# An encoder trunk on one core: the first two chunks of the input projection run side by side, and x, weights and the residual share one queue

## The chip, the core and the metric

The kernel runs on one core of a Trainium2 chip. A core has engines that each work through their own instructions in order: TensorE (PE: matmuls, with PEld its weight loads), VectorE (DVE), ScalarE (ACT), GpSimd (POOL) and SyncE (SP). SP, ACT and POOL also issue transfers (DMA) between the chip's memory and the core's own memory; a transfer that has to wait for something holds up whatever stands behind it on the engine that issues it. Matmul results collect in eight banks (PSUM). The metric is the device time of one execution in microseconds; the number given is the median of several runs.

## The reference

Two encoder layers on 256 tokens of width 2048, in float32. Each layer has an attention part and an MLP part, each ahead of a norm over the width. Layer 0 uses differential attention (12 heads, two softmaxes subtracted), layer 1 windowed attention with a sink; in both, four more heads attend to 256 memory tokens. A relative-position bias table is shared. Cut to what matters here:

```
h = rms_norm(x, norm_attn[i])
proj = h @ w_in_a[j]                              # 2048 x 5120 in layer 0
q, k, v, q_m = split(proj, [1536, 3072, 4608])
q = rms_norm(q per head half, a_q_norm[j]);  k = rms_norm(k per head half, a_k_norm[j])
o = diff_attention(q, k, v, positions, rel_bias, lam, 64 ** -0.5)
...
x = x + heads @ w_out[i]
h = rms_norm(x, norm_mlp[i])
x = x + square(relu(h @ w_up[i])) @ w_down[i]
```

## The kernel before

**Precision.** Every float32 factor is split into a rounded part `hi` and a rest `lo`, and a product is made of three matmuls: x_hi w_hi, x_hi w_lo, x_lo w_hi. For weights, ScalarE makes `hi` (L184) and VectorE `lo` (L185); for x, ScalarE multiplies by the norm's gain and rounds (L200) and VectorE makes the rest (L201). The norm's factor per token is not needed for that; it is applied to the results, from statistics over the tokens (`row_stats`, into `st0`).

**Weights.** Every weight matrix is cut into chunks of 512 columns, and each chunk into eight pieces of 512 KB: 128 partitions x 1024 floats, which are two k tiles (128 rows of the contraction each) of 512 columns. `plan` lists all pieces in the order of use; `fetch` takes the next one, issues its transfer on SP's queue (L183) and its two conversions; `piece` keeps up to three pieces fetched (AHEAD = 2). The raw piece, `hi` and `lo` have four buffers each.

**A chunk of a projection** (`chunk_tok`) takes two banks, one for each 128 tokens, and for each piece runs 2 k tiles x 2 token tiles x 3 matmuls = 12 matmuls (L276 to L278). Eight pieces make 96 matmuls.

**The first chunk** (chunk 6 of layer 0, values of the first four heads) is special: `lead=first` makes each piece come in two halves of 256 KB, and before each half prepares one k tile of x: `load_x` issues the transfers of x on ScalarE's queue (L724; block 0 in two parts of 128 KB, the others, two k tiles each, 256 KB), and `make_x2` converts. So during the first chunk all of x and the chunk's weights have to arrive. The second chunk (chunk 0, queries) needs only weights.

**The residual.** `xt`, x by tokens, is loaded in four parts of 512 KB on SP's queue (L730, task `loads`), each placed behind the last weight transfer (`issue_after(behind[0])`). From it come the statistics: `chunk_sq` (L234) four times, then `start_stats`, which also copies the value chunk out of its banks.

**Side work.** A list of `Task`s holds everything that isn't a chunk: `tick` counts one and runs the first task step that is due and whose predecessors are done; `tick(2)` runs two. Each piece ends with a tick. Tasks of the start: the scalars (L589 to L602), the preparation of the position bias (`prep`: seven steps, among them position transfers L511 and L513, arithmetic on VectorE from L518, and the table written to memory at L535), eight pairs `bias_hot` (four spread loads on GpSimd's queue, L560, and a comparison, L562) and `bias_rows` (48 small matmuls, L571, into two "aux" banks, copied out by VectorE and ScalarE, L572), then the norms and transposes of q and k (`norm_T`) and the attention heads. PSUM has four banks with the tag "mm" and four with "aux".

A scheduler of the framework places the instructions of each engine, mostly in program order; it can place one that it holds to be ready ahead of one that still waits. Ahead of everything 16 warm-up products run on TensorE (L99; 32 matmul records).

Of the kernel before, what the change touches and what calls it, by code (L numbers as in the profile page):

```python
# [14 lines left out]
F32 = mybir.dt.float32  # L15
# [4 lines left out]
ALU = mybir.AluOpType  # L20
AX = mybir.AxisListType

P = 128
S = 256
D = 2048
KT = D // P
# [7 lines left out]
AHEAD = 2  # L34
# [3 lines left out]
G_ATTN, G_MEM, G_MLP = 0, 2 * KT, 4 * KT  # L38
# [8 lines left out]
def trunk(ctx: ExitStack, tc: tile.TileContext, xin, xtok, memin, pos, rel, gcol, rows,  # L47
          w_a, w_b, w_mem, w_out, w_up, w_down, out):
    nc = tc.nc
# [3 lines left out]
    xp = ctx.enter_context(tc.tile_pool(name="xp", bufs=1))  # L53
# [16 lines left out]
    def blk(shape, dt):  # L70
        return xp.tile(shape, dt, tag="blk", name=nm("blk"), bufs=10)
# [96 lines left out]
    ready = deque()  # L168
    behind = [None]

    def fetch(parts=1, lead=None):

        name, c, j = plan.popleft()
        src = weights[name][c, j]
# [3 lines left out]
        n = 1024 // parts  # L178
        for i in range(parts):
            s = slice(i * n, (i + 1) * n)  # L180
            if lead is not None:
                lead(i)
            behind[0] = nc.sync.dma_start(raw[:, s], src[:, s])  # L183
            nc.scalar.copy(hi[:, s], raw[:, s])  # L184
            nc.vector.tensor_tensor(lo[:, s], raw[:, s], as32(hi)[:, s], op=ALU.subtract)  # L185
        ready.append(((name, c, j), hi, lo))

    def piece(name, c, j, lead=None):

        if lead is not None:  # L190
            fetch(2, lead)
        else:
            while plan and len(ready) <= AHEAD:
                fetch()
        key, hi, lo = ready.popleft()
        assert key == (name, c, j), (key, name, c, j)
        return hi, lo
# [44 lines left out]
    def row_stats(st):  # L242
        e1 = mean_sq()
        nc.vector.tensor_scalar_mul(st[:, 0:2], e1, EPS)
        inv_sqrt(st[:, 2:4], e1, 2)
# [15 lines left out]

        return Task([lambda: two(0), lambda: two(1)], wait=1, gap=1)

    def chunk_tok(w, c, X2, before=None, lead=None, steps=1):
        ps = [bank("mm") for _ in range(2)]
        for j in range(8):
            if before is not None:
                before(j)
            hi, lo = piece(w, c, j, lead and (lambda i: lead(2 * j + i)))
            for kk in range(2):  # L270
                for t in range(2):
                    k = 2 * j + kk
                    ws = slice(kk * 512, kk * 512 + 512)
                    xh = X2[k][:, 0, t * P:(t + 1) * P]
                    xl = X2[k][:, 1, t * P:(t + 1) * P]
                    nc.tensor.matmul(ps[t], lhsT=xh, rhs=hi[:, ws], start=(k == 0), stop=False)  # L276
                    nc.tensor.matmul(ps[t], lhsT=xh, rhs=lo[:, ws], start=False, stop=False)  # L277
                    nc.tensor.matmul(ps[t], lhsT=xl, rhs=hi[:, ws], start=False, stop=(k == KT - 1))  # L278
            tick(steps)
        return ps  # L280

    def chunk_out(w, c, nj, x2_of, tag, steps=1):
        ps = [bank(tag) for _ in range(4)]
# [28 lines left out]
    def norm_T(ps, st, nseg, g, before=None):  # L312

        dim = 512 // nseg
        qn = []
        hi = blk([P, 4, S], F32R)
        lo = blk([P, 4, S], F32R)

        def rows():
            ms = small(2 * nseg)  # L320
            rs = small(2 * nseg)
            for t in range(2):
                sq = t2k([P, 512])
# [395 lines left out]
    def load_x(j):  # L719
        if j < 8:  # L720
            xs[j] = xp.tile([P, 2, S], F32, tag="h2", name=nm("xs"), bufs=12)
            for k in range(2 * j, 2 * j + 2) if j == 0 else (2 * j,):
                n = 1 if j == 0 else 2
                nc.scalar.dma_start(xs[j][:, k - 2 * j:k - 2 * j + n, :],  # L724
                                    xin[:, S * k:S * (k + n)].rearrange("p (k s) -> p k s", s=S))

    def load_residual(c):
        cs = slice(c * 512, (c + 1) * 512)
        with tc.issue_after(behind[0].ins):
            nc.sync.dma_start(xt[:, :, cs], xtok.rearrange("p (t d) -> p t d", t=2)[:, :, cs])  # L730

    def first(k):
        if k == 0:
            load_x(0)
        elif k == 1:
            load_x(1)
            load_x(2)
        elif k % 2 == 0:
            load_x(k // 2 + 2)
        X2[k] = make_x2(xs[k // 2][:, k % 2, :], gc[:, G_ATTN + k:G_ATTN + k + 1])  # L740

    bias = big([P, 12, 2, S])
    Task([scalars], wait=4)
# [2 lines left out]
    rows_done = [Task([lambda i=i: bias_hot(i), lambda i=i: bias_rows(i, bias)], [prep], wait=BW) for i in range(8)]  # L746
    Task([lambda: bias_save(bias)], rows_done)
    H2 = [None] * KT
    loads = Task([lambda c=c: load_residual(c) for c in range(4)], wait=5, gap=2, front=True)
    for g in range(3):  # L750
        ps = chunk_tok("a", 6 + g, X2, lead=first if g == 0 else None)
        steps = 2 if g == 0 else 1
        v = blk([P, 2, 512], F32)
        if g == 0:
            def start_stats(v=v, ps=ps):
                row_stats(st0)
                val_f32(v, ps, st0)

            Task([lambda c=c: chunk_sq(c) for c in range(4)] + [start_stats], (loads,), gap=1, front=True)
        else:  # L760
            val_f32(v, ps, st0)
        ps = chunk_tok("a", g, X2, steps=steps)
        qT, qd = norm_T(ps, st0, 8, gs[:, 0:1])
        ps = chunk_tok("a", 3 + g, X2)
        kT, kd = norm_T(ps, st0, 8, gc[:, G_AK:G_AK + 1])
        for h in range(4):
            Task(diff_head(h, qT, kT, v, bias, H2, 4 * g + h), [qd, kd] + rows_done)
    ps = chunk_tok("a", 9, X2)
    qm, qd = norm_T(ps, st0, 4, gs[:, 2:3])
    mem_part(0, qm, qd, H2)  # L770
# [79 lines left out]
```

## Time and profile before

| | us |
|---|---|
| median of 3 runs (lowest to highest) | 2149.51 (2148.49 to 2150.24) |
| profiled execution | 2150.42 |
| its span | 2148.6 |
| TensorE busy in the span | 2137.6 |
| VectorE, ScalarE, GpSimd busy | 1315.6, 1083.6, 35.7 |
| granted TensorE clock | 1.0 |
| moved by transfers | 409.24 MB, mean 190 GB/s |

The span runs from the first to the last instruction of the profiled execution; the execution's own time lies a little over it. Lines of the profile name the source line (L277), the engine, the operation, the output and the inputs by their names in the kernel (`mm<-lo,x`: a matmul into a bank tagged "mm" from `lo` and x), the shapes, the count, and where given the idle time of the engine just before, with what ended it. "raw" is a weight piece as it arrives, "xs" a block of x, "xt" the residual, "rw" the scalars' rows.

### The profile page before, as it was taken

Reading aid. Unit: us, or ns where it says so; the run is one execution under the profiler, and the core shown is the slowest. Engines: PE = TensorE matmul, PEld = TensorE weight load, DVE = VectorE, ACT = ScalarE, POOL = GpSimd, SP = SyncE. Lnnn points to the kernel's source line nnn. Section 1 sums busy time; section 2 is a strip of 40 time slices with the busy share of each in tenths; the row PEclk is TensorE's granted clock in tenths of the full one; section 3 lists DMA queues with packets and bytes.
Section 4 is the critical chain, followed back from the end, with each engine's and each line's share of the span. In section 5 each row is a group of like instructions: output and inputs, shape, how many; then the busy total and the mean of one; then the engine's idle time right before and its main releaser. Section 6 shows DMA issues by size and latency. Waiting matters only on the chain.

```text
span 2148.6 us, 29416 instructions
## 1 busy us (share of the span) xinstructions
PE 2137.6 (99%) x11116; PEld 1806.4 (84%) x11116; DVE 1315.6 (61%) x2067; ACT 1083.6 (50%) x1740; POOL 35.7 (2%) x61
## 2 busy tenths in 40 slices
PE   9999999999999999999999999999999999999999
PEld 7877878888888888888888888888888888888887
DVE  7667786565555555566556677655555556556554
ACT  6456675454444445555545566554444444544443
POOL 1200020000000000000000000000000000000000
PEclk9999999999999999999999999999999999999999
DMA  8865565666666666666656656566666666666654
GB/s 292 237 209 154 157 195 153 187 183 189 185 194 188 191 186 193 193 195 235 198 194 192 181 167 178 155 183 183 185 195 188 192 189 185 196 196 212 192 193 148
DMA packets 114959, 409.24 MB, mean 190 GB/s; under 512 B 13568, under 2 KB 14336, under 8 KB 114560
## 3 DMA queue, kind: packets, MB, share of 16 engines
q1 hardware_dynamic: 111840, 401.01, 60.9%
q0 software_dynamic: 1536, 4.20, 0.8%
q10 hardware_dynamic: 1440, 2.15, 0.3%
q8 instruction: 87, 1.43, 0.3%
q14 instruction: 56, 0.46, 0.1%
HBM read 401.93 MB, written 5.37 MB: 190 GB/s over the span
## 4 chain that ended last, share of the span: by engine, by line
PE 97%; DMA 1%; DVE 1%; ACT 1%; issue 0%; SPq 0%; POOL 0%; ACTq 0%; DVEq 0%; POOLq 0%
PE mm L289 11%; PE aux L289 11%; PE mm L276 9%; PE mm L277 9%; PE mm L278 9%; PE mm L293 6%; PE aux L293 6%; PE mm L680 5%; PE mm L679 5%; PE mm L678 5%; PE aux L679 5%; PE aux L680 5%; PE aux L678 5%; DMA raw<-in_w_a 1%; PE aux L368 1%; PE aux L339 1%
## 5 line engine op out<-in xcount | busy, mean ns | idle before, releaser
L185 DVE TENSOR_TENSOR lo<-raw,hi 128x1024 fp32r<-128x1024 f32 (+1 forms) x744 | 892.7, 1214 | 747.7 <-ACT hi L184 747.3
L184 ACT CAST hi<-raw 128x1024 fp32r<-128x1024 f32 (+1 forms) x744 | 764.3, 1044 | 815.2 <-PE aux L289 194.1
L276 PE MATMUL mm<-hi,x 128*128 128x512 f32 x704 | 281.3, 401 | 2.0 <-ACT hi L184 2.0
L277 PE MATMUL mm<-lo,x 128*128 128x512 f32 x704 | 276.3, 392 | 2.1 <-DVE lo L185 2.1
L278 PE MATMUL mm<-hi,x 128*128 128x512 f32 x704 | 275.9, 392 | 0.0
L289 PE MATMUL mm<-x,hi 128*128 128x512 f32 x1024 | 247.4, 391 | 0.0
L289 PE MATMUL aux<-x,hi 128*128 128x512 f32 x1024 | 246.9, 391 | 0.0
L289 PEld LDWEIGHTS mm<-x,hi 128*128 128x128 f32 x1024 | 188.2, 188 | 36.8 <-DVE xt L642 0.5
L289 PEld LDWEIGHTS aux<-x,hi 128*128 128x128 f32 x1024 | 188.2, 188 | 36.4
L679 PE MATMUL aux<-lo,h 128*128 128x512 f32 x512 | 199.5, 390 | 0.5 <-DVE lo L185 0.5
L680 PE MATMUL aux<-hi,h 128*128 128x512 f32 x512 | 199.2, 389 | 0.0
L678 PE MATMUL aux<-hi,h 128*128 128x512 f32 x512 | 199.2, 389 | 0.0
L678 PE MATMUL mm<-hi,h 128*128 128x512 f32 x512 | 199.2, 389 | 0.0
L679 PE MATMUL mm<-lo,h 128*128 128x512 f32 x512 | 199.2, 389 | 0.0
L680 PE MATMUL mm<-hi,h 128*128 128x512 f32 x512 | 199.2, 389 | 0.0
L276 PEld LDWEIGHTS mm<-hi,x 128*128 128x128 f32 x704 | 132.2, 188 | 29.1 <-ACT hi L184 3.3
L277 PEld LDWEIGHTS mm<-lo,x 128*128 128x128 f32 x704 | 132.6, 188 | 28.2 <-DVE lo L185 4.2
L278 PEld LDWEIGHTS mm<-hi,x 128*128 128x128 f32 x704 | 132.2, 188 | 27.9 <-DVE x L201 0.2
L293 PEld LDWEIGHTS mm<-x,lo 128*128 128x128 f32 x1024 | 131.4, 191 | 4.8
L293 PEld LDWEIGHTS aux<-x,lo 128*128 128x128 f32 x1024 | 131.3, 191 | 5.0
L293 PE MATMUL mm<-x,lo 128*128 128x256 f32 x1024 | 133.3, 283 | 0.0
L293 PE MATMUL aux<-x,lo 128*128 128x256 f32 x1024 | 132.8, 283 | 0.0
(166 smaller groups left out, 2114.8 us busy)
## 6 DMA issues: line engine op xcount, KB each, us to landing
raw<-in_w_up SPq DMA_DIRECT2D x256, 512.0 KB, 3.9
raw<-in_w_down SPq DMA_DIRECT2D x256, 512.0 KB, 4.2
raw<-in_w_a SPq DMA_DIRECT2D x72, 512.0 KB, 4.0
raw<-in_w_out SPq DMA_DIRECT2D x64, 512.0 KB, 3.6
raw<-in_w_b SPq DMA_DIRECT2D x48, 512.0 KB, 3.7
raw<-in_w_mem SPq DMA_DIRECT2D x32, 512.0 KB, 3.8
raw<-in_w_a SPq DMA_DIRECT2D x16, 256.0 KB, 5.7
blk<-bkt POOLq DMA_DIRECT2D x32, 128.0 KB, 8.8
```

Of the source, the lines that this page charges most:

```text
L184: nc.scalar.copy(hi[:, s], raw[:, s])
L185: nc.vector.tensor_tensor(lo[:, s], raw[:, s], as32(hi)[:, s], op=ALU.subtract)
L276: nc.tensor.matmul(ps[t], lhsT=xh, rhs=hi[:, ws], start=(k == 0), stop=False)
L277: nc.tensor.matmul(ps[t], lhsT=xh, rhs=lo[:, ws], start=False, stop=False)
L278: nc.tensor.matmul(ps[t], lhsT=xl, rhs=hi[:, ws], start=False, stop=(k == KT - 1))
L289: nc.tensor.matmul(ps[o], lhsT=hi[:, cols(k % 2, o)], rhs=x2.rearrange("p a s -> p (a s)"), start=(k == 0), stop=(k == 2 * nj - 1))
L293: nc.tensor.matmul(ps[o][:, 256:512], lhsT=lo[:, cols(k % 2, o)], rhs=x2[:, 0, :], start=False, stop=False)
L339: nc.tensor.transpose(out=pt[:, h * P:(h + 1) * P], in_=qn[t][:, h * P:(h + 1) * P], identity=ident)
L368: nc.tensor.transpose(out=pt[:, kt * S + qt * P:kt * S + (qt + 1) * P], in_=p_of(qt)[:, kt * P:(kt + 1) * P], identity=ident)
L678: nc.tensor.matmul(ps[n][t], lhsT=xh, rhs=hi[:, ws], start=(k == 0), stop=False)
L679: nc.tensor.matmul(ps[n][t], lhsT=xh, rhs=lo[:, ws], start=False, stop=False)
L680: nc.tensor.matmul(ps[n][t], lhsT=xl, rhs=hi[:, ws], start=False, stop=(k == 4 * KT - 1))
```

## The change

Four things change, all before the third chunk of layer 0.

1. *Two chunks side by side.* `chunk_pair("a", 6, 0, ...)` works on the value chunk and the query chunk together: `plan` lists their pieces by turns (6, 0, 6, 0, ...), the value chunk's results go to two "mm" banks and the query chunk's to two "aux" banks, and for each k tile the six matmuls of one chunk are followed by the six of the other. There are two ticks per pair of pieces, so 16 ticks as before, now of one step each. The third chunk (chunk 3) runs with two steps per tick.
2. *One queue.* x comes on SP's queue, not ScalarE's. The first pair of pieces comes in halves, with each k tile of x block 0 ahead of the two halves that need it: x, 6, 0, x, 6, 0. Later, x block j + 1 is issued before the pieces that are fetched while pair j runs; a block is converted just before its pair (`next_x`).
3. *The residual* comes in eight parts of 256 KB (one token tile x 512 columns), one for each pair from j = 2, and the last two in the first step of the statistics' task. Each still stands behind the last weight transfer.
4. *Norm and statistics.* The four `chunk_sq` and `start_stats` are a task that begins behind the pair. The query chunk's `norm_T` used to run right behind its chunk; now it is a late step (`norm_T(..., before)`), which waits for the statistics' task, and which stands in the list behind the bias steps. Its two "aux" banks are held until then.

The diff, cut to its core:

```diff
-    for layer, (name, chunks) in enumerate((("a", (6, 0, 3, 7, 1, 4, 8, 2, 5, 9)), ("b", (3, 4, 0, 1, 2, 5)))):
+    plan.extend(("a", c, j) for j in range(8) for c in (6, 0))
+    for layer, (name, chunks) in enumerate((("a", (3, 7, 1, 4, 8, 2, 5, 9)), ("b", (3, 4, 0, 1, 2, 5)))):
...
+    def fetch_part(key, raw, hi, lo, s):
+        name, c, j = key
+        behind[0] = nc.sync.dma_start(raw[:, s], weights[name][c, j][:, s])
+        nc.scalar.copy(hi[:, s], raw[:, s])
+        nc.vector.tensor_tensor(lo[:, s], raw[:, s], as32(hi)[:, s], op=ALU.subtract)
...
+    def fetch(n=1, lead=None):
+
+        new = [new_piece() for _ in range(n)]
+        for i in range(2 if lead else 1):
+            if lead:
                 lead(i)
...
+            for p in new:
+                fetch_part(*p, slice(i * 512, i * 512 + 512) if lead else slice(0, 1024))
+        ready.extend((p[0], p[2], p[3]) for p in new)
...
+    def chunk_pair(w, ca, cb, X2, lead, before):
+
+        pa = [bank("mm") for _ in range(2)]
+        pb = [bank("aux") for _ in range(2)]
+        for j in range(8):
+            if j == 0:
+                fetch(2, lead)
+            else:
+                before(j)
+            two = [(pa, *piece(w, ca, j)), (pb, *piece(w, cb, j))] if j else [(pa, *ready.popleft()[1:]), (pb, *ready.popleft()[1:])]
+            for kk in range(2):
+                for ps, hi, lo in two:
+                    mms_tok(ps, 2 * j + kk, hi, lo, X2)
+            tick()
+            tick()
+        return pa, pb
...
-            for k in range(2 * j, 2 * j + 2) if j == 0 else (2 * j,):
-                n = 1 if j == 0 else 2
-                nc.scalar.dma_start(xs[j][:, k - 2 * j:k - 2 * j + n, :],
-                                    xin[:, S * k:S * (k + n)].rearrange("p (k s) -> p k s", s=S))
-
-    def load_residual(c):
-        cs = slice(c * 512, (c + 1) * 512)
+            nc.sync.dma_start(xs[j], xin[:, 2 * S * j:2 * S * j + 2 * S].rearrange("p (k s) -> p k s", s=S))
+
+    def load_residual(i):
+
+        c, t = i // 2, i % 2
         with tc.issue_after(behind[0].ins):
-            nc.sync.dma_start(xt[:, :, cs], xtok.rearrange("p (t d) -> p t d", t=2)[:, :, cs])
...
+            nc.sync.dma_start(xt[:, t, c * 512:(c + 1) * 512], xtok[:, t * D + c * 512:t * D + (c + 1) * 512])
...
+    def next_x(j):
+        if j == 1:
+            load_x(1)
+        load_x(j + 1)
+        take_x(2 * j)
+        take_x(2 * j + 1)
+        if j > 1:
+            load_residual(j - 2)
...
-    loads = Task([lambda c=c: load_residual(c) for c in range(4)], wait=5, gap=2, front=True)
...
+    pv, pq = chunk_pair("a", 6, 0, X2, first_x, next_x)
+    v = blk([P, 2, 512], F32)
+
+    def start_stats(v=v):
+        row_stats(st0)
+        val_f32(v, pv, st0)
+
+    stats = Task([lambda: (load_residual(6), load_residual(7))] + [lambda c=c: chunk_sq(c) for c in range(4)] + [start_stats],
+                 gap=1, front=True)
+    qT, qd = norm_T(pq, st0, 8, gs[:, 0:1], lambda: None)
+    qd.after.append(stats)
...
+        ps = chunk_tok("a", 3 + g, X2, steps=1 if g else 2)
```

`mms_tok` is the old loop body of `chunk_tok` (L276 to L278) as a function of its own, and `first_x` issues and converts the two k tiles of x block 0.

More of the change, by code (lines that the diff above doesn't have):

```diff
@@ L169, in trunk, with new_piece @@
     behind = [None]
-    def fetch(parts=1, lead=None):
-        name, c, j = plan.popleft()
-        src = weights[name][c, j]
+    def fetch_part(key, raw, hi, lo, s):
[3 more added lines that the diff above has]
+        nc.vector.tensor_tensor(lo[:, s], raw[:, s], as32(hi)[:, s], op=ALU.subtract)
+    def new_piece():
         raw = wp.tile([P, 1024], F32, tag="raw", name=nm("raw"))
@@ L177, in fetch, with piece @@
         lo = wp.tile([P, 1024], F32R, tag="lo", name=nm("lo"))
[L178 to L181, printed above, removed]
-                lead(i)
[L183 to L194, printed above, removed]
+        return plan.popleft(), raw, hi, lo
+    def fetch(n=1, lead=None):
+        new = [new_piece() for _ in range(n)]
+        for i in range(2 if lead else 1):
+            if lead:
+                lead(i)
+            for p in new:
+                fetch_part(*p, slice(i * 512, i * 512 + 512) if lead else slice(0, 1024))
+        ready.extend((p[0], p[2], p[3]) for p in new)
+    def piece(name, c, j):
+        while plan and len(ready) <= AHEAD:
+            fetch()
         key, hi, lo = ready.popleft()
@@ L262, in to_features, with mms_tok, chunk_tok @@
         return Task([lambda: two(0), lambda: two(1)], wait=1, gap=1)
-    def chunk_tok(w, c, X2, before=None, lead=None, steps=1):
+    def mms_tok(ps, k, hi, lo, X2):
+        ws = slice((k % 2) * 512, (k % 2) * 512 + 512)
+        for t in range(2):
+            xh = X2[k][:, 0, t * P:(t + 1) * P]
+            xl = X2[k][:, 1, t * P:(t + 1) * P]
+            nc.tensor.matmul(ps[t], lhsT=xh, rhs=hi[:, ws], start=(k == 0), stop=False)
+            nc.tensor.matmul(ps[t], lhsT=xh, rhs=lo[:, ws], start=False, stop=False)
+            nc.tensor.matmul(ps[t], lhsT=xl, rhs=hi[:, ws], start=False, stop=(k == KT - 1))
+    def chunk_tok(w, c, X2, before=None, steps=1):
         ps = [bank("mm") for _ in range(2)]
@@ L268, in chunk_tok @@
                 before(j)
-            hi, lo = piece(w, c, j, lead and (lambda i: lead(2 * j + i)))
+            hi, lo = piece(w, c, j)
             for kk in range(2):
[L271 to L278, printed above, removed]
+                mms_tok(ps, 2 * j + kk, hi, lo, X2)
             tick(steps)
         return ps
+    def chunk_pair(w, ca, cb, X2, lead, before):
[9 more added lines that the diff above has]
+                for ps, hi, lo in two:
+                    mms_tok(ps, 2 * j + kk, hi, lo, X2)
+            tick()
+            tick()
+        return pa, pb
     def chunk_out(w, c, nj, x2_of, tag, steps=1):
@@ L721, in load_x, with take_x, first_x @@
             xs[j] = xp.tile([P, 2, S], F32, tag="h2", name=nm("xs"), bufs=12)
-            for k in range(2 * j, 2 * j + 2) if j == 0 else (2 * j,):
-                n = 1 if j == 0 else 2
-                nc.scalar.dma_start(xs[j][:, k - 2 * j:k - 2 * j + n, :],
-                                    xin[:, S * k:S * (k + n)].rearrange("p (k s) -> p k s", s=S))
-    def load_residual(c):
-        cs = slice(c * 512, (c + 1) * 512)
+            nc.sync.dma_start(xs[j], xin[:, 2 * S * j:2 * S * j + 2 * S].rearrange("p (k s) -> p k s", s=S))
+    def load_residual(i):
+        c, t = i // 2, i % 2
         with tc.issue_after(behind[0].ins):
-            nc.sync.dma_start(xt[:, :, cs], xtok.rearrange("p (t d) -> p t d", t=2)[:, :, cs])
-    def first(k):
+            nc.sync.dma_start(xt[:, t, c * 512:(c + 1) * 512], xtok[:, t * D + c * 512:t * D + (c + 1) * 512])
+    def take_x(k):
+        X2[k] = make_x2(xs[k // 2][:, k % 2, :], gc[:, G_ATTN + k:G_ATTN + k + 1])
+    def first_x(k):
         if k == 0:
-            load_x(0)
-        elif k == 1:
-            load_x(1)
[L737 to L740, printed above, removed]
+            xs[0] = xp.tile([P, 2, S], F32, tag="h2", name=nm("xs"), bufs=12)
+        nc.sync.dma_start(xs[0][:, k, :], xin[:, S * k:S * k + S])
+        take_x(k)
+    def next_x(j):
+        if j == 1:
+            load_x(1)
+        load_x(j + 1)
[3 more added lines that the diff above has]
+            load_residual(j - 2)
     bias = big([P, 12, 2, S])
@@ L748, in trunk @@
     H2 = [None] * KT
-    loads = Task([lambda c=c: load_residual(c) for c in range(4)], wait=5, gap=2, front=True)
-    for g in range(3):
[L751 to L760, printed above, removed]
+    heads_of = lambda g, qd, kd, qT, kT, v: [Task(diff_head(h, qT, kT, v, bias, H2, 4 * g + h), [qd, kd] + rows_done) for h in range(4)]
+    pv, pq = chunk_pair("a", 6, 0, X2, first_x, next_x)
[7 more added lines that the diff above has]
+    qd.after.append(stats)
+    for g in range(3):
+        if g:
+            ps = chunk_tok("a", 6 + g, X2)
+            v = blk([P, 2, 512], F32)
             val_f32(v, ps, st0)
-        ps = chunk_tok("a", g, X2, steps=steps)
-        qT, qd = norm_T(ps, st0, 8, gs[:, 0:1])
-        ps = chunk_tok("a", 3 + g, X2)
+            ps = chunk_tok("a", g, X2)
+            qT, qd = norm_T(ps, st0, 8, gs[:, 0:1])
+        ps = chunk_tok("a", 3 + g, X2, steps=1 if g else 2)
         kT, kd = norm_T(ps, st0, 8, gc[:, G_AK:G_AK + 1])
-        for h in range(4):
-            Task(diff_head(h, qT, kT, v, bias, H2, 4 * g + h), [qd, kd] + rows_done)
+        heads_of(g, qd, kd, qT, kT, v)
     ps = chunk_tok("a", 9, X2)
```

## The prediction

> **What bounds the kernel now.** I read the page's totals first, then the groups of matmuls by line in two stretches of the start, then TensorE's timeline there, and last what ScalarE and VectorE waited for. The totals leave little to win:
>
> ```profile
> span 2148.6 us, 29416 instructions
> PE 2137.6 (99%) x11116; PEld 1806.4 (84%) x11116; DVE 1315.6 (61%) x2067; ACT 1083.6 (50%) x1740; POOL 35.7 (2%) x61
> ```
>
> TensorE sets the end, and the change adds no matmul and takes none away. So only time in which TensorE stands still can be won, and the page shows 2148.6 - 2137.6 = 11.0 us of it. TensorE's timeline says where the start has its share (columns: start, duration, engine, line, operation, count, idle before and its releaser):
>
> ```profile
> 6.17 0.50 PE L276 MATMUL mm<-hi,x 128*128 128x512 f32 x1
> ...
> 8.57 0.74 PE L276 MATMUL mm<-hi,x 128*128 128x512 f32 x2 [0.67 <-ACT hi L184]
> ...
> 11.04 0.73 PE L276 MATMUL mm<-hi,x 128*128 128x512 f32 x2 [0.55 <-ACT hi L184]
> ...
> 15.41 0.50 PE L277 MATMUL mm<-lo,x 128*128 128x512 f32 x1 [0.61 <-DVE lo L185]
> ...
> 21.45 0.73 PE L276 MATMUL mm<-hi,x 128*128 128x512 f32 x2 [0.76 <-ACT hi L184]
> ...
> 26.67 0.50 PE L277 MATMUL mm<-lo,x 128*128 128x512 f32 x1 [1.46 <-DVE lo L185]
> ...
> 61.74 1.38 PE L571 MATMUL aux<-tab,blk 128*128 128x48 bf16 x48
> ```
>
> Five pauses, 4.05 us of idle time in all, every one inside the first chunk, which needs x and weights at once. But busy time is modelled and hides the pipeline's refill after each pause, so I count matmuls instead. Groups by line and shape, first from 6.17 to 26.67 us, then from there to the first bias matmul at 61.74 us:
>
> ```profile
> L277 PE MATMUL mm<-lo,x 128*128 128x512 f32 x20 | 8.3, 414 | 0.6 <-DVE lo L185 0.6
> L276 PE MATMUL mm<-hi,x 128*128 128x512 f32 x22 | 8.1, 411 | 2.0 <-ACT hi L184 2.0
> L278 PE MATMUL mm<-hi,x 128*128 128x512 f32 x20 | 7.9, 396 | 0.0
> ```
>
> ```profile
> L277 PE MATMUL mm<-lo,x 128*128 128x512 f32 x52 | 20.4, 391 | 1.5 <-DVE lo L185 1.5
> L278 PE MATMUL mm<-hi,x 128*128 128x512 f32 x52 | 20.3, 390 | 0.0
> L276 PE MATMUL mm<-hi,x 128*128 128x512 f32 x50 | 19.4, 389 | 0.0
> ```
>
> The second stretch has 154 matmuls in 61.74 - 26.67 = 35.07 us: 0.2277 us each, without a gap. (62 + 154 = 216 is 18 weight pieces of 12, so no record is missing.) At that pace the first 62 need 14.1 us; they took 26.67 - 6.17 = 20.5. **The start loses 6.4 us**, and that is all this change can win there.
>
> What TensorE waited for goes back to transfers that stand at the head of an in-order engine. From ScalarE's and VectorE's timelines:
>
> ```profile
> 7.50 0.51 ACT L200 ACTIVATE x<-xs,gc 128x256 fp32r<-128x256 f32 x1 [1.38 <-DMA xs<-in_xin]
> ...
> 20.38 0.51 ACT L200 ACTIVATE x<-xs,gc 128x256 fp32r<-128x256 f32 x1 [4.21 <-DMA xt<-in_xtok]
> ```
>
> ```profile
> 13.74 0.29 DVE L592 TENSOR_TENSOR t1k<-rw 128x128 f32<-128x128 f32 x1 [1.03 <-DMA rw<-in_rows]
> ...
> 24.47 0.43 DVE L518 CAST t2k<-t2k 128x512 f32<-128x512 int32 x1 [1.35 <-POOL t2k L516]
> ```
>
> The 4.21 us is ScalarE held up by its own next x load, which waited for a 512 KB residual transfer; the casts of weights stood behind it. The last one is the position arithmetic, ahead of weight work on VectorE.
>
> **The change, part by part.** *Pairing.* Two chunks take 2 x 96 matmuls x 0.2277 = 43.7 us, before as after. But a block of x (two k tiles) now feeds 24 matmuls, 5.46 us, not 12. The first chunk before had to bring 4.19 MB of weights, 2.10 MB of x and half the residual in about 22 us of matmuls; after, the pair brings 8.39 MB of weights, 2.10 of x and 1.6 of residual in 43.7 us: 276 GB/s against some 330 before. What the transfers really moved, by stretches (the last column; the third column is GpSimd's busy time):
>
> ```profile
> 0.00:5.00 5.00, 1.14 (x10) 1.00 0.58 175
> 5.00:10.00 5.00, 0.00 (x0) 1.00 0.96 353
> 10.00:15.00 5.00, 0.00 (x0) 1.00 1.03 322
> 15.00:20.00 5.00, 0.00 (x0) 1.00 0.96 315
> 20.00:25.00 5.00, 1.19 (x2) 1.00 0.79 244
> 25.00:30.00 5.00, 0.00 (x0) 1.00 0.90 280
> 30.00:35.00 5.00, 0.00 (x0) 1.00 0.93 275
> 35.00:40.00 5.00, 0.00 (x0) 1.00 0.99 378
> 40.00:45.00 5.00, 0.00 (x0) 1.00 0.91 340
> ```
>
> Summed: 0.88 MB by 5 us, 2.64 by 10, 4.25 by 15, 5.83 by 20, 7.05 by 25, 8.45 by 30, 9.82 by 35, 11.71 by 40, 13.41 by 45. I lay the new order of transfers on this curve. Preparing a landed piece costs (groups of the first 53 us):
>
> ```profile
> L185 DVE TENSOR_TENSOR lo<-raw,hi 128x1024 fp32r<-128x1024 f32 x10 | 12.2, 1222 | 3.2 <-ACT hi L184 3.2
> ...
> L184 ACT CAST hi<-raw 128x1024 fp32r<-128x1024 f32 x10 | 10.5, 1051 | 3.5 <-DVE t1k L534 1.7 <-DMA raw<-in_w_a 1.7 <-PE mm L278 0.2
> ...
> L200 ACT ACTIVATE x<-xs,gc 128x256 fp32r<-128x256 f32 x16 | 8.1, 507 | 8.8 <-DMA xs<-in_xin 4.3 <-DMA xt<-in_xtok 4.2 <-DMA rw<-in_rows 0.4
> ```
>
> I add 0.5 us from moved to landed (an estimate between 0 and 1), then 1.05 for hi and 1.22 for lo. The pair starts no sooner than 6.17, because the warm-up matmuls (L99) hold TensorE to about then; x and first halves (0.45 MB) are there by 5. Pair j, chunk A, starts at 6.17 + 5.46 j, chunk B 1.37 later. Piece A1 ends at 2.41 MB: 9.35 us, lo ready at 12.1; wanted at 11.9. B1, at 2.94 MB: 10.9, lo at 13.7; wanted at 13.2, or 13.5 with A1's delay. So 0.5 us late in all, and two refills of 0.4 (6.4 less the 4.05 shown, over six starts): **1.3 us**. From j = 2: B2, with the scalars' rows, at 4.12 MB, ready 17.4, wanted 18.7; B3 at 5.83 MB, 22.8 against 24.2; B4 at 7.40, 29.0 against 29.6; B5 at 8.97, 34.7 against 35.1; B6 39.7 against 40.5; B7 at 12.12 MB, 44.0 against 46.0. In time throughout, but at B4 and B5 by tenths, so L592 or L518, still ahead of weight work on VectorE, can cost something: between 0 and the 1.03 and 1.35 us they blocked; I take half of their mean, **0.6**, since ScalarE and VectorE now have two conversions of x per 5.46 us, not per 2.73, and catch up.
>
> *x on SP's queue, nine issues gone from ScalarE's.* The head of 4.21 us disappears with the issue that waited. SP pays the nine issues and four more for the residual, and its weights stand behind them:
>
> ```profile
> 30.04 0.55 SPq L730 DMA_DIRECT2D xt<-in_xtok  x1
> ```
>
> 13 x at most 0.55 = 7.2 us over the 44 us of the pair. An issue of 256 KB each 0.55 us would be 477 GB/s, over anything the stretches show, so I cost it at nothing; the cover is the transfer time itself. Without it, up to 0.55 us per issue.
>
> *The residual in eight.* The bytes are the same. In the stretch from 5 to 10 us everything in flight was 128 or 256 KB, and it moved 353 GB/s, the best of the first seven stretches; so 256 KB costs nothing more. [...]
>
> *Statistics and the q chunk's norm moved behind the pair.* The same instructions, later; chunk 3 now runs two task steps per piece. Its two banks are the free pair of "mm", so TensorE needs nothing from them for 8 pieces (21.8 us). What is late next: the q banks stay taken until the bias rows are through (third rival).
>
> **The sum.** 6.4 - 1.3 - 0.6 = 4.5 us. The rest of the program has the same matmuls; I leave its 7 us of idle time as it is. Span 2148.6 - 4.5 = 2144.1. The profiled execution took 2150.4 us, 1.8 outside its span and 0.9 above the median of the runs; so a median of 2149.5 - 4.5 = **2145.0 us**.
>
> **Rivals.** *The transfers are never late.* Stretches from 35 to 45 us show 340 to 378 GB/s where SP was seldom held back; at 340 from 10 us on only A1's 0.25 us and its refill stay. Gain 6.4 - 0.7 = 5.7: 2143.8. Against it: the single queue has no more bytes per us than the two had.
>
> *The stall moves behind the pair.* The bias tables' steps come two ticks of the pair sooner (side at tick 10, not 12), so their 32 spread loads on GpSimd's queue start near 41 us, not 49:
>
> ```profile
> 49.33 4.04 POOL L560 DMA_DIRECT2D blk<-bkt  x8 [24.89 <-DMA bkt<-t1k]
> ```
>
> ```profile
> q1 hardware_dynamic: 1390, 5.06, 57.5%
> ...
> blk<-bkt POOLq DMA_DIRECT2D x32, 128.0 KB, 8.8
> ```
>
> Those rows (the second, transfers from 49 to 81 us) say that beside them SP's queue got 5.06 MB in 32 us, 158 GB/s. Chunk 3 wants 0.524 MB per 2.73 us, 192, and the last 0.8 MB of residual falls there too. With B7 in by 41 us, the fifth and sixth pieces of chunk 3 come at about 66 and 69 us, some 1 us late each: 2.4 us with refills. Gain 4.5 - 2.4 = 2.1: 2147.4. The same time comes out if x runs ahead on SP while weights wait for buffers: four early blocks, 1.05 MB at 315 GB/s, 3.3 us, less 1.3 of slack at B2. For: pieces stand at tenths of slack. Against: each bias row step gives TensorE 1.22 us of other work.
>
> *The banks of "aux".* The pair's q half holds two of four aux banks until its norm runs, behind all eight bias row steps in the list. Each step fills two banks; with two free, step i+1 must wait until the copies of step i are out. Before:
>
> ```profile
> 65.12 0.55 DVE L572 COPY big<-aux 128x384 f32<-128x384 f32 x1
> ```
>
> ```profile
> 65.78 1.38 PE L571 MATMUL aux<-tab,blk 128*128 128x48 bf16 x48
> ```
>
> The first step's copy ended at 65.67, the next step began at 65.78: with two banks it would have been in time by 0.1 us. If ScalarE or VectorE come 1.5 us later at each of seven hand-overs, TensorE loses 10.5 us: 2149.5 - 4.5 + 10.5 = 2155.5. It decides from 4.5 / 7 = 0.64 us per hand-over. Against: the wait before the copy came from the q norm on VectorE, which is moved away.
>
> **How the numbers follow.** Forecast 0.46; never late 0.17; stall moved 0.25; banks 0.12. About 0.2%, 4.3 us, is what a measurement tells from no change, so faster means below 2145.2. The forecast (2143.8 to 2146.3 by its own terms) lies there six times in ten, "never late" always: 0.28 + 0.17, and 0.02 from a small moved stall, 0.47. Slower is the banks' 0.12 with 2153.8 as its bound; the rest, 0.41, is the same. The range goes from 2142.7, where the whole 6.4 us and run noise come together, to 2150.5, which takes in the moved stall at twice its size.
>
> **What would show it.** After the change: 192 matmuls of L276 to L278's successors in about 45.5 us from 6.2; pauses only near 12 to 14 us; no ScalarE wait on a residual transfer; x and weights on one queue at about 290 GB/s to 40 us. Wrong, if pauses add up to over 3 us in the pair, if TensorE stands before pieces of chunk 3 or before bias rows, or if the pair starts after 6.5 us.

## The result: 0.5% slower, and the profile after

| | before | after |
|---|---|---|
| median, us (lowest to highest; 6 runs each, side by side) | 2149.88 (2148.15 to 2152.26) | 2161.45 (2159.95 to 2162.9) |
| ratio, 95% interval | | 1.0054 [1.0041, 1.0067] |
| span of the profiled execution, us | 2148.6 | 2159.5 |

The forecast was 2145.0 with a range to 2150.5. The time is 11.6 us above before and lies outside the range, on the side to which the prediction gave 0.12. The page's totals, after:

```profile
span 2159.5 us, 29393 instructions
PE 2141.2 (99%) x11116; PEld 1810.2 (84%) x11116; DVE 1316.5 (61%) x2061; ACT 1084.5 (50%) x1734; POOL 34.2 (2%) x61
```

The matmuls are the same 11116. Busy time rose by 3.6 us and idle time by 7.3 (from 11.0 to 18.3): 10.9 us more span. Where it lies is read by holding the same points of the program side by side (starts of matmuls in the two timelines, us):

| point | before | after | difference |
|---|---|---|---|
| first matmul of the projection | 6.17 | 7.40 | +1.2 |
| 193rd, the first of chunk 3 | 56.29 | 55.29 | -1.0 |
| first matmul of the first MLP's `up` | 427.8 | 439.6 | +11.8 |
| end of the span | 2148.6 | 2159.5 | +10.9 |

So the pair is a little ahead, and then 12.8 us are lost between the start of chunk 3 and the MLP. What TensorE waited for in the first 120 us of after (columns: the waiting instruction, what it waited for, us in total, times, the longest):

```profile
PE aux L593 <- DVE big L594: 7.9, 1, 7.9
PE mm L273 <- DVE lo L176: 2.1, 3, 0.8
PE aux L593 <- ACT big L594: 0.8, 1, 0.8
PE aux L273 <- DVE lo L176: 0.8, 1, 0.8
PE mm L272 <- ACT hi L175: 0.5, 2, 0.3
```

And TensorE's timeline of after (start, duration, line, operation, count, idle before and its releaser; L593 are the bias rows' matmuls, L571 before):

```profile
7.40 0.47 PE L272 MATMUL mm<-hi,x 128*128 128x512 f32 x1
...
14.18 0.50 PE L273 MATMUL mm<-lo,x 128*128 128x512 f32 x1 [0.53 <-DVE lo L176]
...
46.96 0.49 PE L272 MATMUL mm<-hi,x 128*128 128x512 f32 x1 [0.31 <-ACT hi L175]
...
48.22 0.50 PE L273 MATMUL mm<-lo,x 128*128 128x512 f32 x1 [0.77 <-DVE lo L176]
...
50.89 0.50 PE L273 MATMUL aux<-lo,x 128*128 128x512 f32 x1 [0.76 <-DVE lo L176]
...
55.29 0.49 PE L272 MATMUL mm<-hi,x 128*128 128x512 f32 x1 [0.21 <-ACT hi L175]
...
56.55 0.50 PE L273 MATMUL mm<-lo,x 128*128 128x512 f32 x1 [0.76 <-DVE lo L176]
...
59.18 1.38 PE L593 MATMUL aux<-tab,blk 128*128 128x48 bf16 x48
...
62.99 0.39 PE L274 MATMUL mm<-hi,x 128*128 128x512 f32 x1
71.26 1.12 PE L593 MATMUL aux<-tab,blk 128*128 128x48 bf16 x24 [7.88 <-DVE big L594]
73.22 1.12 PE L593 MATMUL aux<-tab,blk 128*128 128x48 bf16 x24 [0.85 <-ACT big L594]
...
74.74 0.63 PE L273 MATMUL mm<-lo,x 128*128 128x512 f32 x1
...
79.05 1.38 PE L593 MATMUL aux<-tab,blk 128*128 128x48 bf16 x48
```

Three things stand in it. From 7.40 to 46.7 us the pair runs with one pause, at 14.18, as forecast for its second pieces. Then there are five pauses from 46.96 to 56.55. Then one standstill of 7.88 us ahead of the second bias step, with a second wait of 0.85 behind it. The stretch from 63.22 (62.99 plus one matmul of 0.23, where the second bias step would have begun) to 79.05 takes 15.83 us; it holds one bias step and 12 matmuls, which at the pace of before take 1.22 + 12 x 0.2277 = 3.95. The difference, **11.9 us, is nearly the whole loss**; the rest is the pause at 56.55, inside chunk 3's first piece (1.26 us from its first matmul to its second, not 0.23).

**The first cause: SP's queue.** Waits and timeline of SP in after; L557 writes the bias table to memory, L563 loads the relative biases, L744 is x, L750 the residual, L174 weights:

```profile
SPq L557 <- DVE x L204: 4.7, 1, 4.7
```

```profile
31.75 1.35 SPq L563 DMA_DIRECT2D tab<-in_rel  x3
37.45 0.40 SPq L557 DMA_DIRECT2D bkt<-t1k  x1
38.41 0.42 SPq L744 DMA_DIRECT2D xs<-in_xin  x1
38.87 0.43 SPq L750 DMA_DIRECT2D xt<-in_xtok  x1
39.40 0.85 SPq L174 DMA_DIRECT2D raw<-in_w_a  x2
```

The table write stands on SP's queue at a place that SP reaches at 33.1 us, and its data is ready on VectorE at 37.4 (L556, 36.73 + 0.69 us; the list of waits names L204, which VectorE ran next to it). For over 4 us (4.7 by the list of waits) SP issues nothing, and behind the write stand the last block of x, a residual part and weights. What that does to the transfers, and when it reaches the engines (windows of after: window, length, TensorE's busy time and matmuls, granted clock, DMA share, GB/s; then ScalarE's timeline):

```profile
30.00:35.00 5.00, 5.00 (x24) 1.00 0.93 300
35.00:40.00 5.00, 5.00 (x24) 1.00 0.16 39
40.00:45.00 5.00, 5.00 (x24) 1.00 0.95 294
```

```profile
41.63 0.91 ACT L203 ACTIVATE x<-xs,gc 128x256 fp32r<-128x256 f32 x2 [4.76 <-DMA xs<-in_xin]
...
65.53 0.63 ACT L237 ACTIVATE t2k<-xt 128x512 f32<-128x512 f32 x1 [1.59 <-DMA xt<-in_xtok]
```

39 GB/s between 300 and 294: some 1.3 MB come late, ScalarE stands for the last block of x, and the five pauses follow. Before, the same write (L535) was issued at 45.62 us and waited 0.3 us for its data (SP's timeline and its waits):

```profile
45.62 0.38 SPq L535 DMA_DIRECT2D bkt<-t1k  x1
```

```profile
SPq L535 <- DVE t1k L534: 0.3, 1, 0.3
```

**The second cause: what VectorE does in order.** The spread loads of the bias tables follow the table write, on GpSimd's queue; they began at 49.33 before and begin here at

```profile
39.58 4.03 POOL L582 DMA_DIRECT2D blk<-bkt  x8 [14.96 <-DMA bkt<-t1k]
```

So they share the transfers with the pair's last weights and the last two parts of the residual, which were late already. VectorE's timeline then (L176 the weights' rests, L241 the statistics, L584 the comparison of a spread table, L594 the copy of a bias step out of its bank):

```profile
66.28 0.16 DVE L241 TENSOR_REDUCE sm<-ssq 128x2 f32<-128x8 f32 x1 [3.20 <-ACT t2k L237]
...
66.86 0.75 DVE L584 TENSOR_SCALAR blk<-blk,itf 128x2048 bf16<-128x2048 bf16 x1
...
69.51 1.23 DVE L176 TENSOR_TENSOR lo<-raw,hi 128x1024 fp32r<-128x1024 f32 x1 [1.90 <-ACT hi L175]
70.66 0.55 DVE L594 COPY big<-aux 128x384 f32<-128x384 f32 x1
```

The copy at 70.66 empties a bank that the first bias step had filled by about 60.5. It stands behind a reduction that waits for the last residual part and behind a weight rest that waits for its piece. Neither has any business with the bias step; they only stand ahead of the copy on VectorE. The comparison at 66.86 waits for no transfer of its own; it stands behind the same reduction, and it makes the second bias step's own input (the first three comparisons are at 50.76, 66.86 and 77.39, the first matmuls of the first three steps at 59.18, 71.26 and 79.05). So even with free banks that step could not have begun before 66.86 + 0.75 = 67.6, 4.2 us into the standstill.

**The third: the clock.** Windows of after again, two of 2 us:

```profile
68.00:70.00 2.00, 0.00 (x0) 0.58 1.00 264
...
78.00:80.00 2.00, 2.00 (x42) 0.86 1.04 285
```

TensorE stood still from 63.4, the granted clock went from 1.0 to 0.5 at about 68.3 (0.58 over 2 us is 0.16 of it at 1.0) and came back within the second of these windows, at about 78.5. The matmuls of this stretch follow each other by 0.43 us (74.74 to 75.17) and not by 0.2277: for 10 of them 2 us more, over half of the 3.6 us of added busy time.

### The profile page after: what moved, and what is told of

The parts are those of the page before. It is cut to its first block, busy times and chain, and to the rows that moved or that the text cites. A ratio compares the mean times of both kernels' runs of the same rounds, so it can differ in the third digit from the quotient of the medians.

```text
span 2159.5 us, 29393 instructions
## 1 busy us (share of the span) xinstructions
PE 2141.2 (99%) x11116; PEld 1810.2 (84%) x11116; DVE 1316.5 (61%) x2061; ACT 1084.5 (50%) x1734; POOL 34.2 (2%) x61
## 3 DMA queue, kind: packets, MB, share of 16 engines
HBM read 401.93 MB, written 5.37 MB: 189 GB/s over the span
## 4 chain that ended last, share of the span: by engine, by line
PE 96%; DMA 2%; DVE 1%; ACT 0%; issue 0%; SPq 0%; POOL 0%; ACTq 0%; DVEq 0%; POOLq 0%
PE mm L311 11%; PE aux L311 11%; PE mm L272 9%; PE mm L274 9%; PE mm L273 9%; PE mm L315 6%; PE aux L315 6%; PE aux L702 5%; PE aux L700 5%; PE mm L700 5%; PE mm L701 5%; PE aux L701 5%; PE mm L702 5%; DMA raw<-in_w_a 2%; PE aux L390 1%; PE aux L361 1%
## 5 line engine op out<-in xcount | busy, mean ns | idle before, releaser
L176 DVE TENSOR_TENSOR lo<-raw,hi 128x1024 fp32r<-128x1024 f32 (+1 forms) x738 | 891.9, 1223 | 756.0 <-ACT hi L175 755.4
L272 PE MATMUL mm<-hi,x 128*128 128x512 f32 x672 | 271.0, 404 | 0.5 <-ACT hi L175 0.5
L273 PE MATMUL mm<-lo,x 128*128 128x512 f32 x672 | 264.1, 393 | 2.1 <-DVE lo L176 2.1
L274 PE MATMUL mm<-hi,x 128*128 128x512 f32 x672 | 264.5, 394 | 0.0
L274 PEld LDWEIGHTS mm<-hi,x 128*128 128x128 f32 x672 | 126.7, 189 | 26.9
L273 PEld LDWEIGHTS mm<-lo,x 128*128 128x128 f32 x672 | 127.2, 189 | 26.1 <-DVE lo L176 3.1
L272 PEld LDWEIGHTS mm<-hi,x 128*128 128x128 f32 x672 | 126.9, 189 | 26.0 <-ACT hi L175 1.6
```

## The experiments

The theory after the result: the table write holds up SP's queue, which eats the pair's lead; then the earlier spread loads and VectorE's order make the standstill, and the halved clock prices it. The rival is the prediction's third: the pair's query half holds two "aux" banks, and L593 waits before L594 because banks are short.

**e1: the table write on another queue.**

```
-        nc.sync.dma_start(bkt.rearrange(...), bb)      # L557
+        nc.gpsimd.dma_start(bkt.rearrange(...), bb)
```

> The bias table's write to memory (line 557) goes from SP's queue to GpSimd's, nothing else. In the changed kernel SP stood 4.7 us before this write, the transfers fell to 39 GB/s from 35 to 40 us, and TensorE paused five times between 46 and 57 us (about 4.4 us with refills). Queue theory: x, weights and residual behind the write come 4 us sooner, the five pauses go, the last residual lands sooner, so the wait before the second bias rows (7.9 us) shrinks by 4 as well: 2161.5 - 4.4 - 4 = about 2153. Bank theory alone: only the pauses go, the long wait stays: about 2157. Load theory (weights, residual and spread loads ask for more than the transfers move, whatever the order): the pauses come back a few us later: 2160 or more.

Measured: 2152.80 us, 1.0015 [1.0006, 1.0024], 8.65 us below after. Its windows (TensorE), its TensorE timeline and its VectorE timeline:

```profile
35.00:40.00 5.00, 5.00 (x23) 1.00 0.89 269
...
54.00:55.00 1.00, 0.00 (x0) 0.59 1.02 201
55.00:60.00 5.00, 4.75 (x11) 0.50 1.01 258
```

```profile
51.57 0.39 PE L272 MATMUL mm<-hi,x 128*128 128x512 f32 x1
...
55.25 0.80 PE L273 MATMUL mm<-lo,x 128*128 128x512 f32 x1 [3.29 <-DVE lo L176]
```

```profile
53.31 0.75 DVE L584 TENSOR_SCALAR blk<-blk,itf 128x2048 bf16<-128x2048 bf16 x1 [8.51 <-DMA blk<-bkt]
```

The transfers move 269 GB/s where after moved 39, and the pair reaches chunk 3 at 51.57, 4.7 us ahead of before, though it began 1.0 later (7.18 against 6.17). But the lead is lost right there: VectorE stands 8.51 us before the comparison of a spread table that is still on its way, three weight rests stand behind it, TensorE waits 3.29 us, and its clock halves once more. The 7.9 us wait is gone without a bank being freed. That the time meets the queue theory's 2153 is in part luck: by its sum the long wait was to shrink by 4 us, but it is gone, and a new wait with a halved clock has come. The spread loads, which follow the write, also begin 3.5 us later than in after (43.09 against 39.58), so the 8.65 us cannot be put down to the queue alone.

**e2: the query half's banks emptied at once; e3: that and e1.**

```
+    qc = blk([P, 2, 512], F32)
+    nc.scalar.copy(qc[:, 0, :], pq[0])
+    nc.vector.tensor_copy(qc[:, 1, :], pq[1])
-    qT, qd = norm_T(pq, st0, 8, ...)
+    qT, qd = norm_T([qc[:, 0, :], qc[:, 1, :]], st0, 8, ...)
```

> The query chunk's two banks are copied out at once behind the pair (one copy on ScalarE, one on VectorE, 0.6 us each) and its norm reads the copies, so four aux banks are free for the bias rows. Bank theory: the waits of 7.9 and 0.8 us before the second bias rows and the halved clock behind them (2.2 us) go; TensorE then waits only for weights of chunk 3's fourth piece, some 3 to 4 us: 2161.5 - 11.9 + 3.5 = about 2153. Queue or load theory: the bank wait only shows where TensorE would have stood anyway; a wait for weights of about the same length appears at 65 to 71 us: 2158 to 2161.

> Both edits: table write on GpSimd's queue and the query banks copied out. If banks and queue are the whole loss: 2161.5 - 11.9 - 4.4 = about 2145, below the kernel before. Load theory: waits for weights of 3 to 6 us stay between 50 and 72 us: 2149 to 2152.

Measured: e2 2163.63, 1.0066 [1.0049, 1.0083]; e3 2151.68, 1.0017 [1.0007, 1.0026]. In e2 TensorE has four free banks and no longer waits for a copy. It waits for something else (waits of TensorE):

```profile
PE aux L593 <- DVE blk L584: 9.4, 2, 4.7
```

Two waits of 4.7 us for the comparison stand where the wait of 7.9 for the copy stood, and the time is no better. The first is at the second bias step, whose comparison again runs right behind the statistics (67.97 us, their reduction at 67.39). So the shortage of banks decided which instruction was named, not how long TensorE stood. e3 stays with e1: waits of 3.6 us for the comparison, 2.3 for a weight rest. Of its expectations the one that both together give the forecast fell, and the load theory's time (2149 to 2152) came: with SP's queue and the banks out of the way, what is left is that spread loads run too early and VectorE stands for them.

**e4: x back on ScalarE's queue.**

```
-            nc.sync.dma_start(xs[j], ...)
+            nc.scalar.dma_start(xs[j], ...)
...
-        nc.sync.dma_start(xs[0][:, k, :], ...)
+        nc.scalar.dma_start(xs[0][:, k, :], ...)
```

> The changed kernel with x back on ScalarE's queue (nine issues), pairing, order of pieces, residual in eight and late norm as they are. If the single queue is where x is held up behind the table write, x block 7 comes in time and ScalarE is not held for 4.8 us at 41 us, but the weights are still behind the write: pauses of 46 to 57 us down by 1 to 2 us, 2159 to 2160. If the queue of x does not matter: 2161.5. If x on ScalarE's queue waits for other transfers as it did before (4.2 us once): 2163 or more. The long wait before the bias rows stays in all three.

Measured: 2157.33, 1.0043 [1.0028, 1.0058], 4.1 us below after, and more than expected. With x elsewhere, SP reaches the table write later (it is issued at 41.53 us, in after at 37.45) and waits less for it (waits of SP):

```profile
SPq L557 <- DVE tab L569: 1.4, 1, 1.4
```

The spread loads begin at 45.23, TensorE has no pause between 46 and 57 us, and the bias waits for the copies are 2.9 and 1.0 us, where the expectation had the long wait stay at 7.9. So taking x off the queue removes a part of the trouble, by moving what meets at the write.

**e5: e1, and the preparation four ticks later.** In the pair a tick comes twice per pair of pieces; the preparation's start moves from tick 5 to tick 9.

```
-                  bias_side, bias_table], wait=5, gap=1)
+                  bias_side, bias_table], wait=9, gap=1)
```

> e1 (table write on GpSimd's queue) with the bias preparation begun four ticks later (wait 9, not 5), so that the spread loads start near 50 us, about where they did before the change, when the residual and the pair's weights are in. In e1 the spread loads started at 43.1 us, VectorE stood 8.5 us before their first comparison at 53.3, TensorE 3.3 us before a weight piece behind it, and its clock halved for 5 us (2 us more). Collision theory: those 5.7 us go, and the 4 to 5 us that the pair won by 51 us stay: about 2145 to 2147. Rival, that chunk 3's weights and the bias rows cannot be fed beside the spread loads whenever they run: the wait appears later, 2150 to 2153.

Measured: 2147.03, 0.9993 [0.9984, 1.0003]: 5.8 us below e1 and 14.4 below after, by one number and one queue, though its interval does not part it from before. Its GpSimd timeline and, of its waits of TensorE in the first 120 us, that of the bias steps:

```profile
51.42 4.84 POOL L582 DMA_DIRECT2D blk<-bkt  x10 [4.64 <-DMA bkt<-t1k]
```

```profile
PE aux L593 <- DVE blk L584: 1.6, 3, 0.9
```

The spread loads begin at 51.42, behind the weights of the pair. TensorE's only pauses in the pair are of 0.5 us each, at 12.35 and 13.61. Chunk 3 is reached at 51.36, 4.9 us ahead of before, from the same start (6.18 against 6.17). That is the step in which the forecast had counted 4.5.

**e6: e1, and the comparison moved into the bias step, behind the newest weight rest; e7: e5 and e6 together.**

```
-        nc.vector.tensor_scalar(hot, hot, tabs["iota"][:, 0:1], None, op0=ALU.is_equal)   # in bias_hot
+    def bias_compare(i):                                                                  # called ahead of bias_rows(i)
+        hot = tabs[i].rearrange("p r q -> p (r q)")
+        with tc.issue_after(last_lo[0].ins):
+            nc.vector.tensor_scalar(hot, hot, tabs["iota"][:, 0:1], None, op0=ALU.is_equal)
```

> e1 with the comparison of each spread table made a part of the bias-row step and pinned behind the last weight rest on VectorE; the spread loads stay as early as in e1 (43 us). In-order theory (what cost e1 its 3.3 us and the halved clock was weight work standing behind a comparison on VectorE, not too few bytes): that wait goes, 2152.8 - 5.7 = about 2147. Load theory (too few bytes): the fourth weight piece of chunk 3 comes at the same time, TensorE waits there or before a bias row: 2151 to 2153.

> Both: preparation four ticks later and the comparison pinned. If either cause alone is enough, as e5 or e6 alone: 2144 to 2147; if both are needed, only this one falls below the kernel before (2149).

Measured: e6 2150.52, 1.0007 [0.9997, 1.0016]; e7 **2146.55, 0.9986 [0.9977, 0.9996]**, the one of the two that is clear of before, by 2.7 us. In e6 the 3.29 us wait and the halved clock are gone, since no weight rest stands behind a comparison any more; but the spread loads are as early as in e1, and the waits move to the bias steps (waits of TensorE, L590 the comparison, L599 the copies):

```profile
PE aux L598 <- DVE blk L590: 1.6, 3, 1.0
PE aux L598 <- DVE big L599: 1.5, 1, 1.5
PE aux L598 <- ACT big L599: 1.4, 2, 0.9
```

So e6 lies between the two theories' numbers, and the later preparation (e5, 5.8 us below e1) is worth more than the order on VectorE (e6, 2.3 us below e1). In e7, of the waits in the bias steps 0.7 and 0.3 us are left. Its profiled execution was the slowest of its ten (2148.64), so its row-by-row account is not that of its median.

**e8: after with the later preparation alone; e9: e7 with the query half copied out.**

> The changed kernel with the bias preparation four ticles later (wait 9) and the table write left on SP's queue: one number changed. If the write costs because SP stands in line before it while x, weights and residual of the running pair wait behind, then with all of the pair's transfers ahead of it the time alone cures most: within 2 us of e5 (2147). If a write on SP's queue costs wherever it stands (chunk 3's weights and the last residual are behind it now), 4 to 6 us are lost to it: 2151 to 2154.

> e7 (table write on GpSimd's queue, preparation late, comparison pinned) with the query banks copied out at once. Bank theory in what is left of it: the two banks held still cost, and 1 to 2 us go: about 2145. If the banks hold up nothing once transfers and VectorE are in time: 2146.5, the same as e7, or 1 us more for the two copies.

Measured: e8 2149.64, 1.0002 [0.9992, 1.0012]; e9 2146.70, 0.9989 [0.9980, 0.9999]. e8 is after with one number changed (`wait=5` to `wait=9`), and it takes back 11.8 us, all that the change had cost, with x, weights and the write still on one queue. Its time lies between the two expectations. The write still holds up SP (waits of SP in e8):

```profile
SPq L557 <- DVE t1k L556: 2.6, 1, 2.6
```

That its median lies 2.6 us over e5's is not shown to come from this: its runs spread from 2146.9 to 2151.8, and the profiled one, which has this wait, took 2147.49, hardly more than e5's median. What the slower ones lost is not seen. In e9 no bias step waits at all, and it is no faster than e7: the banks hold up nothing that can be measured once the work comes in time.

**e10 and e11: two parts of the change alone, on the kernel before.** e10 loads the residual in eight blocks, e11 issues x on SP's queue:

```
-            nc.sync.dma_start(xt[:, :, cs], ...)
+            for t in range(2):
+                nc.sync.dma_start(xt[:, t, cs], xtok[:, t * D + c * 512:t * D + (c + 1) * 512])
```

```
-                nc.scalar.dma_start(xs[j][:, ...], ...)
+                nc.sync.dma_start(xs[j][:, ...], ...)
```

> The kernel before with the residual in eight transfers of 256 KB, not four of 512, nothing else. Prediction's step: 256 KB costs nothing more than 512: 2149 to 2150. [...]

> The kernel before with its nine x transfers on SP's queue, chunks one after the other. If the queue of x is worth something by itself (ScalarE's 4.2 us head behind a residual transfer goes): 2146 to 2148. If x and the first chunk's weights simply need more bytes than come: 2149 to 2150. If SP's in-order waits for weight buffers hold x back: 2151 or more.

Measured: e10 2151.15, 1.0007 [0.9997, 1.0016]; e11 2150.72, 1.0004 [0.9994, 1.0013]. Neither can be told from no change; e10's median lies above the 2149 to 2150 that was expected, and its interval, from 0.6 us below before to 3.4 above, leaves open whether the eight transfers cost something. e11 has the pauses in another place: its TensorE timeline shows a bias step (L571) waiting for a comparison.

```profile
75.06 1.53 PE L571 MATMUL aux<-tab,blk 128*128 128x48 bf16 x48 [3.03 <-DVE blk L562]
```

In this profile the table write is issued at 35.88 us and the spread loads begin at 41.82 (before 45.62 and 49.33), though nothing in the preparation was edited. So moving x alone brings the preparation forward, as far as one profile can show it, and a comparison comes late at the same spot without the pair.

**e0: before once more, for the start.** After starts 1.2 us later than before, and the prediction had named a start behind 6.5 us as a sign against it.

> The kernel before, unchanged, for a second profile. Its first profile has the 32 warm-up records in 5.26 us and the first real matmul at 6.17 us; all five profiles of the change and its variants have 6.1 to 6.6 us and a start at 7.4. If the warm-up's length is chance, this profile can show 6 us or more; if the change causes it, it shows 5.3 us again, and the change loses 1.2 us at its very start.

Measured: 2150.37, span 2148.6, as the first time. Its TensorE timeline begins

```profile
1.06 6.06 PE L99 MATMUL aux<-ones 128*128 128x128 f32 x32 [1.06 <-DVE tab L539]
```

where the first profile's 32 warm-up records took 5.26 us. Over all the profiles of this case they took 5.26 to 6.59, in no order with the edits (after 6.59, e5 5.37, e8 5.76, e11 5.41). So the later start is no part of the change, as far as these profiles show; and in the kernel before, which waits for data there, it cost the span nothing. In this second profile the clock halved in the kernel before, too: from 26.2 to 29.6 us, behind one pause of 2.07 us (last section).

## Why the prediction was wrong, step by step

**The loss in the start: right.** 6.4 us by counting matmuls, of which the pair was to keep 4.5. From the first projection matmul to chunk 3 e5 takes 45.18 us, e1 44.39, before 50.12; forecast 45.5, least possible 43.7. After itself takes 47.89, since the table write's pauses fall into it. The pair feeds TensorE as worked out, and in e5 its only pauses are at the second pieces, near 12 to 14 us; the 0.6 us for L592 or L518 does not show. The 0.5 us from moved to landed in the pair's 1.3 us of loss is the author's estimate, which no run shows; with it the rest of piece A1 was to be ready at 12.1 us, and in e5 the matmul that waits for it runs at 13.61, after 0.47 and 0.53 us of idle time at that piece.

**The residual in eight, at nothing: not contradicted.** e10 alone cannot be told from no change; its interval allows up to 3.4 us.

**x on SP's queue, at nothing: the step that failed first.** It priced the issues (0.55 us each) and named the transfer time as cover. It looked at what each issue costs, not at what else stands on that queue. The table write was on it before, too, but there x came by another queue and the write's data was ready. In after SP stood 4.7 us at the write with the last x, the residual and weights behind it; e1, which moves only this write, gives 8.65 us (and later spread loads with it). Neither x nor the write on SP's queue costs this much by itself: e8 keeps both there and e11 has both, and neither can be told from before. It is the write coming while the pair's last transfers stand behind it, and e11 shows that the move of x itself brings the write forward. The row of the write was in the trace of before, with a wait of 0.3 us, and wasn't read. By the price of issues alone e1 should have gained about 0.4 us, the one issue (an estimate, from its row of 0.40 in after); it measured 8.65, and the price of an issue holds nothing of the 4.7 us that SP waited at the write.

**The statistics and the rest of the program, left as they are: the step that failed in size.** "The same instructions, later" overlooked VectorE's order. Behind the pair, statistics, comparisons, weight rests and bias copies meet on it, and the newest copy waits for all that stands ahead of it: for the last residual part and for a weight piece. That is the 7.88 us, and with the second wait and the clock 11.9, where the prediction had put nothing.

**The second rival had the place and the trigger, not the price.** "The stall moves behind the pair", since the spread loads start sooner (forecast near 41 us, seen at 39.58): e5 and e8 show just this, since a later preparation takes back 5.8 us beside e1 and 11.8 beside after. It was priced at 2.4 us because it counted bytes: who gets how many GB/s. It left out that one late transfer at the head of an in-order engine holds up the work behind it (in e1 VectorE stood 8.51 us for one, with three weight rests behind it), and that the clock halved behind the standstill (about 2 us more in after and in e1).

**The third rival had the wait, not the cause.** It named the bias steps waiting for the copies (L593 for L594 in after) and 2155.5 us, nearest to the result. That nearness is chance: it had 1.5 us at each of seven hand-overs, and the trace has 7.88 and 0.85 us at one. With four banks free (e2) the time is no better, and once the work comes in time (e9 against e7) the banks change nothing. A right name in the list of waits is not yet a right cause: the bank was only the last in a chain of things that were late.

**What remains.** Once the write is off SP's queue, the preparation late and the comparison behind the weight rests, the median is 2146.55, 1.6 us above the forecast and 2.7 below before. The pair's lead at chunk 3 (4.5 us in e7's profile) shrinks to 1.4 at the `up` matmuls; its waits and refills explain about 2 of these 3 us in a profiled execution that was slower than its median, and about 1 us stays open. Not tried was a form with the preparation later still, nor one that tells apart what the later preparation gives through the spread loads and what through its arithmetic on VectorE.

## What to carry to other kernels

Before work is moved to another in-order queue or to another time, list what that queue and each engine hold around the new place, and for every entry when its data is ready; in these runs an entry of only 128 KB, the table write, held up all behind it while it waited, and cost where that was needed soon (4.7 us of waiting in after, with the pair's last x behind it; in e8 2.6 us, with no loss to be seen in its profile). When a stage gets faster or reordered, tasks that are placed by counted ticks move with it: look up what they issue and what they will meet. And test a named wait by freeing what it names; if another wait of the same length takes its place, the cause lies further up.

## What the runs showed of the hardware that was not expected

In seven of the fourteen profiles the granted clock of TensorE fell from 1.0 to 0.5 behind a standstill, each time for a multiple of 3.41 us. In after no matmul ran from 63.4 us on, the drop came at 68.3, and the clock came back at 78.5, 5.3 us after the matmuls had resumed for good (73.22). In e1 none ran from 52.0 on, the drop came at 54.2 (0.59 over the window from 54 to 55), and the way back took 5.8 us (55.25 to 61.0). While it was halved, the matmuls came 0.43 us apart and not 0.2277 (74.74 to 78.16 in after, 55.84 to 59.68 in e1). This cost about 2 us on top of each of these two stalls, so the stall of 3.29 us in e1 cost more than 5. In the kernel before's second profile (e0) one pause of 2.07 us stood ahead of such a drop (windows of TensorE, as above):

```profile
22.80:26.21 3.41, 1.34 (x7) 1.00 0.80 294
26.21:29.63 3.42, 3.42 (x10) 0.50 0.72 181
```

Read in windows of 0.25 us, the fourteen profiles have ten such drops while the kernel works, all in the first 100 us, and they last 3.41 us (five times: e0, e2, e11, twice in e3), 6.83 (four times: e1, e4, twice in e2) or 10.24 (after), that is one, two or three times 3.41. In the 3.41 us ahead of each drop TensorE stood still for 2.0 us or more (2.04 in e2, 2.07 in e0, 2.21 in e1, all of it in after). In the other steps of 3.41 us, counted back and forth from the drops, that ran at full clock (the first 120 us of these seven profiles) it stood still for 1.5 us or less, and behind the five pauses of under 0.8 us in after the clock stayed at 1.0, as it did behind one pause of 1.61 us in e10.

The 32 warm-up records took 5.26 to 6.59 us from profile to profile, while the granted clock reads 1.0 over them (windows of 0.5 us in before, after, e1, e2 and e4); what makes the difference is not shown.
